# A hybrid decoder layer on one core: half-width recurrence levels, stores on ScalarE's queue, experts tile by tile, four sums held in PSUM

## The chip, the core and the metric

The kernel runs on one core of a Trainium2 chip. The metric is the time of one execution in device microseconds (us). The kernel before takes 2983.25 us, the median of three runs (2981.98 to 2986.4).

The text names the engines as the profile does: PE is TensorE (PEld its weight loads), DVE is VectorE, ACT is ScalarE, POOL is GpSimd, SP is SyncE, which here only issues DMAs (SPq).

## What is computed

One decoder layer over 1024 tokens of width 1024, float32 throughout:

```python
mod = silu(c) @ w_ada + b_ada              # shift/scale/gate of both sub-layers
h = rmsnorm(x) * (1 + scale1) + shift1
proj = h @ w_in
#  columns A: 4 heads x 128, gated linear recurrence with a decay per channel
#     scores[t, s] = sum_d q[t,d] k[s,d] exp(b[t,d] - b[s,d])   for s <= t in a chunk
#  columns B: 4 groups x 128, gated causal convolution of width 3
x = x + gate1 * (concat[A, B] @ w_out)
h = rmsnorm(x) * (1 + scale2) + shift2
#  PEER, per token: 8 heads, top 16 of 128 + 128 keys, top 16 of their sums -> 128 experts of 16384
act = gelu(h . u[expert]);  x = x + gate2 * sum(gate * act * v[expert])
out = rmsnorm(x) * final_norm_w
```

## The kernel before

**Products.** A float32 operand of a large product is split into a high part (a copy on ACT, line 113) and a low part (a subtraction on DVE, line 114); a product is then three matmuls (high.high, high.low, low.high). The weights come through one list `order` in the order of their use: SP loads a block of 512 KB into one of three buffers `wl` (line 201), ACT and DVE split it one or two blocks ahead of PE.

**Token mixing** (`mixing`) runs once for each half of the sequence, 24 blocks of `w_in` each (line 467), and between the blocks the recurrence of four heads. A chunk's 128x128 scores are built in levels: level l (0 to 6) covers the pairs (s, t) whose highest differing bit is l. `level(mask, X, Y)` multiplies four chunks of 128x128 on PE (line 577) and copies the pairs of its mask into `sT` with a predicated copy of 128x512 on DVE (line 578). A head has seven levels and the diagonal. Then the group norms' scales (`finish`, lines 681 and 683), the product with `w_out` (line 714), the residual and norm 2.

**PEER, dense and gathered.** 704 tokens of the second part take all 16384 experts in dense form; the other 320 ("gathered") read their own 128 expert rows each by indirect DMA, in tiles of 128, 128 and 64 tokens. The gathered tokens' queries come after the first half (line 873; scores and queries are stored in DRAM, lines 909 and 913).

**The background.** `background()` is a generator of steps on DVE and POOL: first the top-k of both full tiles (`top16`, `candidates`, `softmax`, `digits`, `pick`), which leaves their expert indices; then per tile 128 rows of `u`, each a gather by POOL (line 1082) and a product with accumulation on DVE (line 1100), and 128 rows of `v` (a gather, line 1092 on DVE), then the norm and the store (`norm_store`). `advance` draws steps in the midst of the other work, so many for each block and stage (`RATES`; the gates stage has 0). The planner that orders each engine's instructions may issue one earlier than its place in the program when its inputs are ready; the products with gathered rows are pinned behind the vector instruction traced before them. The gather of a row can run ahead as far as there are row buffers (five).

**Dense PEER.** Queries and top-k of the dense tokens, with blocks of `u` products (line 1161, two PSUM buffers `pa`, gelu on ACT at line 1166 into `ge`) strewn between; 40 of 128 such blocks are done early and their `ge` stored (`ged`, line 1174). The gates stage (`gates`) builds one-hot products (lines 1312 and 1318 on DVE), 16 matmuls for eight tokens (line 1327, five PSUM buffers `pg`), copies to `stg` on ACT (line 1330), and for each 64 tokens stores 4096 KB (`gd`, line 1335). The main loop takes the other 88 blocks, multiplies by the gates (line 1376), and for each three blocks runs `v_phase`: 16 sums of 128 x 384 or 128 x 320 (line 1395). Two of the sums stay in PSUM for the whole loop (`FIXED`), the other 14 are formed in one of four buffers `pv` and added to SBUF by DVE (line 1411).

**Queues.** SP issues nearly all loads and stores, in order; an issue waits for its buffer or its data and holds what is behind it. POOL issues the gathers and the stores of `x1d` and `h2d`.

Of the kernel before, what the change touches and what calls it, by code (L numbers as in the profile page):

```python
# [7 lines left out]
F32 = mybir.dt.float32  # L8
# [11 lines left out]
P = 128  # L20
# [19 lines left out]
# the gathered tokens of the last, half tile get their experts together with the half tile of the others  # L40
# [4 lines left out]
GB = 2  # L45
# [17 lines left out]
FIXED = [(0, 0), (1, 0)]  # L63
# [34 lines left out]
def build(tc, A, out, dbg=None):  # L98
# [27 lines left out]
    def rsqrt(r, v, tmp, e=0):  # L126
        """of v / 4 ** e: a first guess from the exponent, then Newton steps"""
# [12 lines left out]
    with root:  # L140
# [36 lines left out]
        # ---------------------------------------------------------------- stationary operands  # L177
        # all of [P, KC, P], in the order in which TensorE takes them; each is fetched two and split one ahead
# [24 lines left out]
        def halve(n):  # L203
            """there is a third set of halves at times"""
# [7 lines left out]
        def deepen(pl, first, n, every):  # L212
            """that many more from the first on: one of so many goes into a pool of its own"""
# [18 lines left out]
        def ahead():  # L232
            """in the midst of the products with one: split the next"""
# [5 lines left out]
        # ---------------------------------------------------------------- constants, modulation  # L239
# [4 lines left out]
        # three buffers of four row tiles, in turn of the normalised input or w_out, and of the mix or the residual  # L244
# [36 lines left out]
        # TensorE gets to its full clock while the first loads are under way  # L281
# [29 lines left out]
        def mod_part(sec, wa, d):  # L311
            """some columns of a section of the modulation"""
# [5 lines left out]
        def mod_part_rows(sec, wa, d):  # L318
            """the same on TensorE, as a row that is turned into columns"""
# [28 lines left out]
        # ---------------------------------------------------------------- norm 1 and the values  # L348
# [14 lines left out]
        def lnT1(xs, pl, k, h1, onact=False):  # L363
            """transpose a column block of the four row tiles, scale, shift and split it"""
# [16 lines left out]
        def wi_load(pl, k, lb=3, hb=2, ahead=0, wait=[]):  # L381
            """loads run ahead of the splits"""
# [34 lines left out]
        # ---------------------------------------------------------------- projections, token mixing  # L417
# [6 lines left out]
        # lower bounds  # L424
# [16 lines left out]
        # a window of 32 columns of it holds ones in one of them  # L441
# [12 lines left out]
        def mixing(half, mods, h1, og):  # L454
            """projections, recurrence, convolution and group norms of half a sequence, into og"""
# [43 lines left out]
            # blocks of w_in: per head f, q, g (0..11), per conv group c, x, b (12..23)  # L499
# [54 lines left out]
            # masks of the levels: the highest bit in which s and t differ, for s < t  # L554
# [14 lines left out]
            def hgrn(h):  # L569
# [3 lines left out]
                def level(mask, X, Y):  # L573
# [4 lines left out]
                    V.copy_predicated(sT, masks[mask][:, None, :].to_broadcast([P, HT, P]), ps_)  # L578
# [32 lines left out]
                level(7, kk, q)  # L611
                yield
                for l in range(6, -1, -1):
# [15 lines left out]
                    level(l, X, X)  # L629
# [42 lines left out]
            def finish(g):  # L672
                """the scales of a group, from the rows of all of them"""
# [18 lines left out]
        # ---------------------------------------------------------------- w_out, norm 2  # L692
# [840 lines left out]
```

## Time and profile before

| | |
|---|---|
| median of three runs | 2983.25 us |
| profiled execution, first to last instruction (span) | 2982.4 us |
| PE busy | 2902.0 us (97%) |
| DVE busy | 2524.2 us (85%) |
| ACT busy | 946.0 us (32%) |
| POOL busy | 796.2 us (27%) |
| DMA, mean rate | 238 GB/s, 709.65 MB |

The profile's page gives no other time of the profiled execution than its span; the median of the runs is 0.9 us above it. A busy PE is not PE at its peak, since matmuls overlap and their ends are modelled. The granted clock is 1.0 at 2.4 GHz and 0.5 at 1.2 GHz; a stretch's figure is the mean.

### The profile page before, as it was taken

How to read it: one execution, taken by the hardware profiler on the slowest of the kernel's cores; microseconds unless marked ns; L12 is line 12 of the kernel's file. 1: busy time of each engine (PE TensorE's matmuls, PEld its weight loads, DVE VectorE, ACT ScalarE, POOL GpSimd, SP SyncE). 2: the span in 40 equal slices, each digit the busy share in tenths (PEclk: the TensorE clock that was granted, in tenths of full speed). 3: DMA queues.
4: the chain of work that ended last, by engine and by line, in shares of the span. 5: the costliest groups of instructions: out<-in, count | busy, mean ns of one | idle time of the engine just before them, and what ended most of it. 6: DMA issues, size and time to landing. Idle time of an engine off the chain costs nothing.

```text
span 2982.4 us, 47131 instructions
## 1 busy us (share of the span) xinstructions
PE 2902.0 (97%) x18242; PEld 2750.8 (92%) x18242; DVE 2524.2 (85%) x5314; ACT 946.0 (32%) x1541; POOL 796.2 (27%) x661
## 2 busy tenths in 40 slices
PE   8999999999999999999999999999999999999998
PEld 6887888878999899999999999999999999999997
DVE  6885559988999877568889989889989988989987
ACT  5643655433122444422222222222222221222221
POOL 0000000000000000015454445435545444444450
PEclk8999999989999999999999999999999999999999
DMA  7424342244223577778889888889889888889883
GB/s 269 146 88 142 130 142 71 85 146 147 61 89 108 181 238 241 234 257 299 302 305 335 314 309 327 320 304 336 304 306 325 319 317 318 307 318 332 304 311 128
DMA packets 286898, 709.65 MB, mean 238 GB/s; under 512 B 26513, under 2 KB 124817, under 8 KB 284370
## 3 DMA queue, kind: packets, MB, share of 16 engines
q1 hardware_dynamic: 192994, 365.56, 35.5%
q0 software_dynamic: 93680, 341.09, 32.2%
q8 instruction: 142, 2.33, 0.3%
q14 instruction: 82, 0.67, 0.1%
HBM read 633.65 MB, written 72.88 MB: 237 GB/s over the span
## 4 chain that ended last, share of the span: by engine, by line
PE 64%; DVE 17%; DMA 10%; issue 5%; ACT 2%; POOL 1%; SPq 0%; DVEq 0%; ACTq 0%; POOLq 0%
PE pv L1395 22%; PE pa L1161 19%; PE pp L467 6%; DMA wl<-in_uT 5%; PE pq L873 4%; PE pacc L1395 3%; DVE wl L114 2%; DMA Wl<-ged 2%; PE ps L577 1%; PE pp L873 1%; PE pg L1327 1%; PE pp L378 1%; DVE gacc L1092 1%; PE pp L714 1%; DVE acc L1411 1%
## 5 line engine op out<-in xcount | busy, mean ns | idle before, releaser
L1161 PE MATMUL pa<-h2h,wh 128*128 128x384 f32 (+1 forms) x1840 | 598.4, 325 | 2.7 <-ACT ge L1166 2.6
L1161 PE MATMUL pa<-h2h,wl 128*128 128x384 f32 (+1 forms) x1840 | 593.9, 323 | 0.0
L1161 PE MATMUL pa<-h2l,wh 128*128 128x384 f32 (+1 forms) x1840 | 593.7, 323 | 0.0
L1395 PE MATMUL pv<-Wh,vh 128*128 128x384 f32 (+1 forms) x1792 | 580.6, 324 | 11.7 <-DVE acc L1411 11.1
L1395 PE MATMUL pv<-Wl,vh 128*128 128x384 f32 (+1 forms) x1792 | 577.3, 322 | 0.0
L1395 PE MATMUL pv<-Wh,vl 128*128 128x384 f32 (+1 forms) x1792 | 577.0, 322 | 0.0
L1395 PEld LDWEIGHTS pv<-Wh,vh 128*128 128x128 f32 x1792 | 336.9, 188 | 22.4 <-DVE acc L1411 19.6
L1161 PEld LDWEIGHTS pa<-h2h,wh 128*128 128x128 f32 x1840 | 346.0, 188 | 4.5 <-ACT ge L1166 3.8
L1161 PEld LDWEIGHTS pa<-h2l,wh 128*128 128x128 f32 x1840 | 346.2, 188 | 0.0
L1161 PEld LDWEIGHTS pa<-h2h,wl 128*128 128x128 f32 x1840 | 346.0, 188 | 0.3 <-DVE wl L114 0.3
L113 ACT ACTIVATE Wh<-Wl 128x704 fp32r<-128x704 f32 x128 | 101.6, 793 | 747.8 <-PE pv L1395 588.2
L1395 PEld LDWEIGHTS pv<-Wh,vl 128*128 128x128 f32 x1792 | 337.0, 188 | 0.0
L1395 PEld LDWEIGHTS pv<-Wl,vh 128*128 128x128 f32 x1792 | 336.9, 188 | 0.0
L113 ACT ACTIVATE wh<-wl 128x1024 fp32r<-128x1024 f32 x187 | 198.0, 1059 | 420.8 <-DMA wl<-in_uT 205.2
L114 DVE TENSOR_TENSOR wl<-wl,wh 128x1024 fp32r<-128x1024 f32 x187 | 227.8, 1218 | 97.7 <-ACT wh L113 95.9
L1411 DVE TENSOR_TENSOR acc<-acc,pv 128x320 f32<-128x320 f32 (+1 forms) x574 | 286.1, 513 | 11.6 <-PE pv L1395 11.3
L114 DVE TENSOR_TENSOR vl<-vl,vh 128x1024 fp32r<-128x1024 f32 x128 | 156.0, 1219 | 18.3 <-ACT vh L113 18.2
L113 ACT ACTIVATE vh<-vl 128x1024 fp32r<-128x1024 f32 x128 | 134.6, 1052 | 79.5 <-DMA vl<-in_v 45.4
L467 PE MATMUL pp<-h1h,wh 128*128 128x512 f32 x384 | 156.6, 408 | 0.0
L467 PE MATMUL pp<-h1h,wl 128*128 128x512 f32 x384 | 152.5, 397 | 3.5 <-DVE wl L114 3.4
L1376 DVE TENSOR_TENSOR Wl<-Wl,gsb 128x704 f32<-128x704 f32 x128 | 113.2, 885 | 48.4 <-DMA Wl<-ged 36.9
L467 PE MATMUL pp<-h1l,wh 128*128 128x512 f32 x384 | 152.3, 397 | 0.0
(1778 smaller groups left out, 5978.2 us busy)
## 6 DMA issues: line engine op xcount, KB each, us to landing
wl<-in_uT SPq DMA_DIRECT2D x128, 512.0 KB
vl<-in_v SPq DMA_DIRECT2D x128, 512.0 KB
gd<-stg SPq DMA_DIRECT2D x11, 4096.0 KB
gsb<-gd SPq DMA_DIRECT2D x64, 704.0 KB
wl<-in_win SPq DMA_DIRECT2D x48, 512.0 KB
wa<-in_wada SPq DMA_DIRECT2D x16, 1024.0 KB
wl<-in_wq SPq DMA_DIRECT2D x32, 512.0 KB
ged<-ge SPq DMA_DIRECT2D x40, 352.0 KB
```

Source lines behind the costliest of these rows:

```text
L113: C.activation(hi, src, AF.Copy)
L114: V.tensor_tensor(lo, src, hi.bitcast(F32), op=OP.subtract)
L378: T.matmul(pvs[t], l[:, t * P:(t + 1) * P], r, start=(k == 0 and l is h1[0][k] and r is wi[0]), stop=(k == KC - 1 and l is h1[1][k]))
L467: T.matmul(pp, l[:, k], r[k], start=(i == 0), stop=(i == 3 * KC - 1))
L577: T.matmul(ps_[:, c], X[:, cs_], Y[:, cs_], start=True, stop=True)
L714: T.matmul(pm, l[:, t * P:(t + 1) * P], r, start=(k == 0 and l is yh[k] and r is woh[k]), stop=(k == KC - 1 and l is yl[k]))
L873: T.matmul(pq[:, :m], l[:, k], hs[k, r][:, o:o + m], start=(i == 0), stop=(i == 3 * KC - 1))
L1092: V.scalar_tensor_tensor(ac, r, aw[:, j:j + 1], ac, op0=OP.mult, op1=OP.add))
L1161: T.matmul(pa[:, :n], l[:, k], h2[k, r][:, o:o + n], start=(i == 0), stop=(i == 3 * KC - 1))
L1376: V.tensor_tensor(gv, gv, gs[b // GB][:, :, b % GB], op=OP.mult)
L1395: T.matmul(pv[:, :n], l[:, c * P:(c + 1) * P], r[:, o:o + n], start=(i == 0 and (not fx or b0 == 0)), stop=(i == 3 * (b1 - b0) - 1 and (no ...
L1411: V.tensor_tensor(a, a, pv[:, :n], op=OP.add)
```

## The change

Comments aside, it has four parts.

1. `level` multiplies only the 64 columns t that can belong to a level (its upper halves). Levels 6 and 5 are copied into `sT` by ACT, block by block, without a mask; levels 4 to 0 by the predicated copy of 128x256. The diagonal is as it was.
2. The stores `scd`, `qgd`, `ged` and `gd` are issued by ACT in place of SP.
3. The background goes tile by tile: top-k of tile 0, its experts, top-k of tile 1, its experts, the last tile's experts. Its loads (`scd`, `h2d`, `x1d`, `g2d`, `fnw`) and its stores of `out` are issued by POOL in place of SP. `RATES` are as before.
4. Four sums stay in PSUM in place of two; the buffers of the other sums are in turn one of two `pa` and one of two `pv`.

```diff
-FIXED = [(0, 0), (1, 0)]
+FIXED = [(0, 1), (0, 5), (1, 1), (1, 5)]
...
+                def level(l, X):
+                    L = 1 << l
+                    n = P // (2 * L)
+                    Xv = X.rearrange("p (c n e l) -> p c n e l", n=n, e=2, l=L)
+                    sv = sT.rearrange("p c (n e l) -> p c n e l", e=2, l=L)[:, :, :, 1]
+                    ps_ = bank("ps")[:, :HT * P // 2].rearrange("p (c n l) -> p c n l", n=n, l=L)
+                    for c in range(HT):
+                        T.matmul(ps_[:, c], X[:, c * P:(c + 1) * P], Xv[:, c, :, 1], start=True, stop=True)
+                    if l >= 5:
+                        for i in range(n):
+                            r = slice(2 * i * L, (2 * i + 1) * L)
+                            C.activation(sv[r, :, i], ps_[r, :, i], AF.Copy)
+                    else:
+                        mv = masks[l].rearrange("p (n e l) -> p n e l", e=2, l=L)[:, :, 1]
+                        V.copy_predicated(sv, mv[:, None].to_broadcast([P, HT, n, L]), ps_)
...
-                SY.dma_start(scd[o:o + w, hp - 3:hp + 1], s_[:w, g])
+                C.dma_start(scd[o:o + w, hp - 3:hp + 1], s_[:w, g])
...
-            SY.dma_start(qgd[hp], qT[:, FULL * P:])
+            C.dma_start(qgd[hp], qT[:, FULL * P:])
...
         def background():
             for g in range(FULL):
+                yield from best(g)
+                yield from experts(g)
+            for g in range(FULL, NG):
+                yield from experts(g)
...
-                        SY.dma_start(s_, scd[g * P:(g + 1) * P, hp:hp + 4])
+                        G.dma_start(s_, scd[g * P:(g + 1) * P, hp:hp + 4])
...
-                    SY.dma_start(hx[c * w:(c + 1) * w], h2d[o:o + w])
+                    G.dma_start(hx[c * w:(c + 1) * w], h2d[o:o + w])
...
-                SY.dma_start(ged[e], ge)
+                C.dma_start(ged[e], ge)
...
-                SY.dma_start(gd[:, :, (t * P) // TG + q4].rearrange("g p b t -> p g b t"),
-                             stg.rearrange("p (g b) t -> p g b t", b=GB))
+                C.dma_start(gd[:, :, (t * P) // TG + q4].rearrange("g p b t -> p g b t"),
+                            stg.rearrange("p (g b) t -> p g b t", b=GB))
...
         def new_pv():
-            return psM.tile([P, 512], F32, name="pv", bufs=PV)
+            turn[0] ^= 1
+            if turn[0]:
+                return psU.tile([P, 512], F32, name="pa", bufs=2)
+            return psM.tile([P, 512], F32, name="pv", bufs=2)
```

## Rows read from the trace of the kernel before

**Rows 1.** The page: busy time of the engines; PE and granted clock in 40 slices; the chain that ended last, by engine.

```profile
PE 2902.0 (97%) x18242; PEld 2750.8 (92%) x18242; DVE 2524.2 (85%) x5314; ACT 946.0 (32%) x1541; POOL 796.2 (27%) x661
...
PE   8999999999999999999999999999999999999998
...
PEclk8999999989999999999999999999999999999999
...
PE 64%; DVE 17%; DMA 10%; issue 5%; ACT 2%; POOL 1%; SPq 0%; DVEq 0%; ACTq 0%; POOLq 0%
```

**Rows 2.** Busy time of each engine by stage: the stretch, its length, busy us (and instructions) of PE, PEld, DVE, ACT and POOL, granted clock, DMA share, GB/s. In order: mixing of the first half; its finish and `w_out` up to the residual; queries of the gathered tokens; mixing of the second half; its finish and `w_out` up to the residual; dense candidates and indices; gates; the last early blocks; main loop; end.

```profile
75.00:253.45 178.45, 177.73 (x988) 148.99 (x986) 143.47 (x261) 87.99 (x144) 0.00 (x0) 1.00 0.33 116
253.45:293.00 39.55, 37.93 (x171) 29.37 (x171) 20.72 (x34) 14.59 (x24) 0.00 (x0) 0.91 0.46 163
355.00:420.00 65.00, 62.66 (x429) 61.01 (x430) 20.33 (x20) 27.63 (x62) 0.00 (x0) 1.00 0.53 171
420.00:608.70 188.70, 183.51 (x986) 152.43 (x985) 184.27 (x677) 93.87 (x151) 2.23 (x3) 0.99 0.25 83
608.70:658.00 49.30, 42.89 (x177) 34.24 (x177) 37.84 (x100) 15.95 (x25) 5.03 (x4) 0.79 0.49 164
840.00:978.00 138.00, 131.55 (x794) 128.87 (x792) 134.59 (x595) 33.92 (x52) 0.76 (x1) 0.98 0.31 105
978.00:1260.00 282.00, 269.77 (x2514) 252.44 (x2513) 214.02 (x368) 137.47 (x258) 0.00 (x0) 0.99 0.74 226
1260.00:1280.00 20.00, 20.00 (x126) 19.93 (x125) 3.25 (x3) 3.99 (x7) 0.00 (x0) 1.00 0.99 326
1280.00:2940.00 1660.00, 1645.65 (x10188) 1632.69 (x10187) 1480.87 (x2084) 388.14 (x535) 781.08 (x634) 1.00 0.86 309
2940.00:2982.00 42.00, 33.01 (x223) 28.85 (x221) 28.76 (x94) 10.58 (x28) 0.00 (x0) 0.92 0.26 94
```

**Rows 3.** A level on PE and, for comparison, eight matmuls with a single moving column: instructions in order of time (start, us, engine, line; x16 are eight matmuls, each of two records).

```profile
486.06 1.95 PE L577 MATMUL ps<-X 128*128 128x128 f32 x16
...
766.04 1.95 PE L294 MATMUL sc<-ones,macc 128*128 128x1 f32 x16
```

**Rows 4.** Groups by line and shape (count, busy us, mean ns): the predicated copy of a level, a DVE operation of half its width, an ACT operation of half its width, the weights of the modulation on DVE.

```profile
L578 DVE COPY_PREDICATED sT<-mask,ps 128x512 f32<-128x512 int32 x64 | 47.3, 738 | 2.6 <-PE ps L577 1.9 <-PE po L634 0.6
...
L301 DVE SCALAR_TENSOR_TENSOR macc<-wa,cs,macc 128x1024 f32<-128x1024 f32 x28 | 35.6, 1273 | 0.1
...
L625 ACT ACTIVATE X<-X 128x256 f32<-128x256 f32 x56 | 23.6, 421 | 59.0 <-DVE X L621 58.9
L627 DVE TENSOR_TENSOR X<-X,kk 128x256 f32<-128x256 f32 x56 | 23.3, 417 | 3.0 <-ACT X L625 3.0
```

**Rows 5.** SP's issues in the gates stage, in order of time: a store of gates, and the issue that comes after it.

```profile
1020.85 0.37 SPq L1335 DMA_DIRECT2D gd<-stg  x1
1021.32 12.45 SPq L201 DMA_DIRECT2D wl<-in_uT  x1
...
1096.51 0.37 SPq L1335 DMA_DIRECT2D gd<-stg  x1
1098.49 11.30 SPq L1174 DMA_DIRECT2D ged<-ge  x1
...
1205.86 0.43 SPq L1335 DMA_DIRECT2D gd<-stg  x1
1214.92 5.45 SPq L1174 DMA_DIRECT2D ged<-ge  x1
```

**Rows 6.** Waits in the gates stage (978 to 1260): who waited for whom, us in total, times, longest; ACT's, then PE's.

```profile
ACT wh L113 <- DMA wl<-in_uT: 31.1, 10, 6.7
ACT wxh L113 <- DMA wl<-in_uT: 22.0, 6, 5.3
...
PE pg L1327 <- DVE P L1318: 9.4, 12, 2.6
```

**Rows 7.** The main loop: the additions of a sum on DVE and the two products with gathered rows (groups by shape), and the waits of PE, PEld and DVE between 1280 and 2940.

```profile
L1411 DVE TENSOR_TENSOR acc<-acc,pv 128x384 f32<-128x384 f32 x287 | 153.0, 545 | 0.2 <-PE pv L1395 0.2
...
L1411 DVE TENSOR_TENSOR acc<-acc,pv 128x320 f32<-128x320 f32 x287 | 133.2, 480 | 11.5 <-PE pv L1395 11.1
...
L1100 DVE SCALAR_TENSOR_TENSOR more<-more,hx 128x1024 f32<-128x1024 f32 x63 | 76.7, 1217 | 7.1 <-DMA more<-in_u,idx 7.1
...
PE pv L1395 <- DVE acc L1411: 11.1, 13, 2.1
...
PEld pv L1395 <- DVE acc L1411: 19.6, 30, 2.4
...
DVE grow__26105 L1100 <- DMA hx<-h2d: 3.5, 1, 3.5
```

**Rows 8.** The background's gathers on POOL, in order of time: the first, the last before the gap, the first after it (in brackets POOL's idle time before and what ended it).

```profile
592.95 1.01 POOL L1082 DMA_INDIRECT grow__13586<-in_u,idx  x1 [167.73 <-DVE hx L925]
...
652.22 0.94 POOL L1082 DMA_INDIRECT grow__13726<-in_u,idx  x1 [5.58 <-DVE grow__13586 L1100]
...
1303.88 1.02 POOL L1082 DMA_INDIRECT grow__13747<-in_u,idx  x1 [462.74 <-DVE grow__13654 L1100]
```

More of the change, by code (lines that the diff above doesn't have):

```diff
@@ L571, in hgrn, with diagonal @@
                 bf = b.rearrange("p c t -> p (c t)")
-                def level(mask, X, Y):
+                def diagonal(X, Y):
                     ps_ = bank("ps").rearrange("p (c t) -> p c t", t=P)
@@ L577, in level @@
                         T.matmul(ps_[:, c], X[:, cs_], Y[:, cs_], start=True, stop=True)
[L578 removed]
+                    V.copy_predicated(sT, masks[7][:, None, :].to_broadcast([P, HT, P]), ps_)
+                    advance(0.9 * RATES["B"])
+                def level(l, X):
[13 more added lines that the diff above has]
+                        V.copy_predicated(sv, mv[:, None].to_broadcast([P, HT, n, L]), ps_)
                     advance(0.9 * RATES["B"])
@@ L609, in states @@
                     yield
-                level(7, kk, q)
+                diagonal(kk, q)
                 yield
@@ L628, in hgrn @@
                     V.tensor_tensor(Xv[:, :, 1], Xv[:, :, 1], qv[:, :, 1], op=OP.mult)
-                    level(l, X, X)
+                    level(l, X)
                     yield
@@ L1000, in pick, with norm_store @@
                 yield 3.5
-        def norm_store(pl, o, w, parts, fw, r, sq):
+        def norm_store(pl, o, w, parts, fw, r, sq, queue=None):
             sf = pl.tile([P, 4], F32, name="sf", bufs=3)[:w]
@@ L1011, in norm_store @@
                 V.scalar_tensor_tensor(r[:w, sl], parts[j], sf[:, 2:3], fw[:w, sl], op0=OP.mult, op1=OP.mult)
-            SY.dma_start(out[o:o + w], r[:w])
+            (queue or SY).dma_start(out[o:o + w], r[:w])
         gp = pool(stQ, "gp", side="right")
@@ L1025, in background, with best @@
             for g in range(FULL):
+                yield from best(g)
+                yield from experts(g)
+            for g in range(FULL, NG):
+                yield from experts(g)
+        def best(g):
+            if True:
                 arenas = {a: [gp.tile([P, DM], F32, name=a, bufs=1), 0] for a in ("hx", "gacc", "more")}
@@ L1066, in background, with experts @@
                 V.tensor_copy(gkg[:, sl], gkf)
-            for g, (o, w) in enumerate(GG):
+        def experts(g):
+            if True:
+                o, w = GG[g]
                 c_ = dup(w)
@@ L1120, in background @@
                 x1 = gp.tile([P, DM], F32, name="hx", bufs=1)
-                SY.dma_start(x1[:w], x1d[o:o + w])
+                G.dma_start(x1[:w], x1d[o:o + w])
                 g2, fw = grow(), grow()
-                SY.dma_start(g2, bcast_rows(g2d[0]))
-                SY.dma_start(fw, bcast_rows(A["fnw"]))
+                G.dma_start(g2, bcast_rows(g2d[0]))
+                G.dma_start(fw, bcast_rows(A["fnw"]))
                 for j in range(2):
@@ L1350, in build @@
         fixed = {f: psM.tile([P, 512], F32, name=f"pacc{f[0]}{f[1]}", bufs=1) for f in FIXED}
-        PV = 6 - len(FIXED)
+        turn = [0]
         def new_pv():
-            return psM.tile([P, 512], F32, name="pv", bufs=PV)
+            turn[0] ^= 1
+            if turn[0]:
+                return psU.tile([P, 512], F32, name="pa", bufs=2)
+            return psM.tile([P, 512], F32, name="pv", bufs=2)
         foldps[0] = new_pv
```

2 lines of the change are left out of this document (1 added, 1 removed).

## The prediction, made before the change was run

> **What bounds the kernel now.** I read the page first [rows 1]: PE is busy for 97% of the span and makes 64% of the chain that ended last, DVE is at 85%. So an edit pays only where PE stands idle, or works at the low clock. The stages say where [rows 2]: length less PE's busy time is 14.4 us in the whole main loop (1660 less 1645.65), 12.2 in the gates, 9.0 at the end, 6.5 in the dense candidates, 6.4 in the second half's finish and w_out (at clock 0.79), 5.2 in its mixing. Everything the change can win is in these gaps. The reader should also see DVE's column: 184.3 of 188.7 us in the second half's mixing, but 143.5 of 178.5 in the first half's, which has the same 24 blocks.
>
> **Part 1, half-width levels.** On PE, the 16 records of a level of 128 columns take 1.95 us, and 16 records with one moving column take 1.95 us too [rows 3]. The time does not depend on the columns, so 64 of them cost what 128 did: 0 us. Were a halved matmul half as long, 448 records (the matmuls of the 56 levels of both halves) at 56 ns less each would give 25 us; were it longer through its strided columns, a loss. One column is the nearer row; I take 0.
>
> The Trainium skill (TensorE: Matmul & The Clock Gate, section Back-to-back issue gap) lists 134 cycles for 128 columns and about 60 for up to 64. By it the levels would give some 13 us on PE (estimate: 448 times 74 cycles at 2.4 GHz), and the sum below would be 13 us lower. The one-column rows of this trace speak against it.
>
> On DVE, of 64 copies of 0.738 us [rows 4] the diagonal's 8 stay, 16 go to ACT and 40 halve to about 0.42 (an operation of half the width takes 0.417): 11.8 + 12.7 = 24.5 us less, half of it in each mixing. ACT gets 24 copies of at most 0.42, 10 us in all, beside 88 and 94 us of work in stages of 178 and 189. In the first half PE lacks 0.7 us only: nothing. In the second half it goes into the next sum.
>
> **Part 3, tile by tile, in the second half.** Now the top-k of both tiles lies in the second half: gathers, which need its indices, begin at 593 and pause at 652 [rows 8]. Its price on DVE: mixing 184.3 less (143.5 less 27, the first half's 21 modulation steps of 1.273 [rows 4]) = 68; finish and w_out 37.8 less 20.7 = 17; 85 us for two tiles, 42 each. After the change tile 1's top-k needs the buffers of tile 0's experts and can't come before them. DVE in the mixing falls from 184 by 12 (levels) and some 35 to about 137 of 189, what the first half has. So PE's gap there should fall from 5.2 to the first half's 0.7: **-4.5 us**. The finish and w_out take 49.3 us against 39.55 for the same work without top-k, 9.75 more, part of it through the clock (0.79 against 0.91). Tile 0's rest may still fall there, so I take **-8** of it. Bounds of both together: 0 and -14.3.
>
> **Stores of the gathered queries.** 24 issues move to ACT, which has 27.6 us of work in 65; at SP's 0.37 to 0.43 each [rows 5] that is 10 us beside free time. SP's loads no longer stand behind stores. PE lacks 2.3 us: **-1** (0 to -2.3).
>
> **Dense candidates.** The program's places now put eight or so products with rows of tile 0 (1.22 + 0.08 us each, pinned) in this stage: about 10 us on a DVE that works 134.6 of 138. They stand ahead of candidates and indices, which the gates wait for; PE has early u blocks to fill with. Bounds 0 and +10; I take **+3**. A dozen more go with the last early blocks, where DVE does 3 us in 20, but the DMAs are at 0.99 and a gather may come late, ahead of the first gate products: **+1**, with bounds 0 and +8.
>
> **Part 2, stores in the gates stage.** Today the issue after a store of gates stands 5.5 to 12.5 us in SP's queue [rows 5], as long as the 4096 KB take to drain (about 13 us from 1020.85), and the weights' load is behind it or is itself held. ACT then waits for loads, 53 us in 16 waits, and PE lacks 12.2 us, 9.4 of them for one-hots of a DVE that is behind ACT [rows 2, 6]. With the stores in ACT's queue the loads go past them. I take half of the gap back, **-6** (bound -12). ACT's own new issues, 11 of gates and about 23 of ge at 0.4, are 14 us in a stage where it works 137 of 282. What is queued behind each on ACT: the next copies of `pg`, the gelus, the high parts of the next weights. This holds only if ACT itself is not held as SP was; that is the first rival.
>
> The Trainium skill (DMA: Bandwidth & Descriptors, section Issuing engines are not separate DMA queues) says that DMAs issued by another engine run on the same 16 engines, and that only sequencer time is saved. By it the loads would win nothing from going past, and this term would be 0 in place of -6. No row here has a store issued by ACT; SP's long issues show that sequencer time is just what was lost.
>
> **Part 4 and the main loop.** Two sums fewer go to SBUF in each of 41 phases: 82 additions of 0.513 (mean of 0.545 and 0.480 [rows 7]) = 42 us less on DVE. The 20 products moved ahead take 26 us away, tile 1's top-k brings 42. Net -26 of 1480.9, from 89% to 88% busy. PE's waits for these additions are 11.1 us; the waits for buffers stay as they are, four in turn before and after. Against it stand the changes of tile: `hx` and the first rows are queued on POOL behind the store of the last tile, which waits for its norm; DVE may stand some 5 us twice, against the 3.5 us wait for `hx` today. I take -4 for the first and +2 for the second: **-2** (bounds -11 and +10). The end keeps its chain: 0.
>
> **Sum.** -4.5 - 8 - 1 + 3 + 1 - 6 - 2 = -17.5 from the profiled 2982.4 gives 2964.9; with the 0.9 us by which the runs' median stands above that span, **2966 us**.
>
> **Rivals.**
> First, ACT is held in SP's place. The limit met SP's next issue whatever it was, and on ACT a store of `ge` follows each store of gates. The three ends [rows 5] give 5.5 to 12.5 us a hold; with 8.6 as their middle, 11 stores hold ACT for 95 us. Priced by today's exchange (53 us of waiting ACT for 12.2 of idle PE): 22 us, less the 12.2 that the loads stop costing, +10 in the stage. Priced as lumps: ACT's longest wait, 6.7 us, goes with PE's longest, 2.6 [rows 6], so some 4.1 us are covered, and 11 times the other 4.5 are 50, less 12, +38. In place of -6, the middle of +24 ends at 2996 us: slower. It decides from holds of about 4 us on. For it: the rows on SP. Against it: ACT is free for half of the stage, PE has five `pg` and two `pa` to run ahead, and 16 such waits of ACT have cost PE little more than half a microsecond each.
>
> Second, the main loop pays. Tile 1's top-k, which is not pinned, comes in a clump on a DVE at 88%, as in the second half, where 85 us of it cost PE 14.3: 7 us for 42; and each change of tile stands 5 us longer than taken, less some cover. About +12: 2978 us. For it, PE does wait for DVE there now; against it, DVE is relieved by 42 us in just this loop.
>
> Third, the change doesn't do what it says: DVE's freed time in the second half is filled again, since tile 0's softmax and indices fall due at its finish. Then the -12.5 stays out: 2978 us. Against it: 42 us of top-k in place of 85.
>
> **How the numbers follow.** Forecast 0.55, with its own range 2950 to 2977; ACT held 0.25; the main loop pays 0.12; the second half stays 0.08. All good ends together (-4.5, -9.8, -2.3, 0, 0, -12.2, -11) give 2943; the first rival at its middle, 2996, and 10 of the 14 us to its upper price give the other end: range **2942 to 3006**. A difference of 0.2%, 6 us, is about what a measurement of this kernel can tell. Faster by more: nearly all of the forecast (0.53), a tenth of the first rival, a quarter of the others: 0.61. Within: a fifth of the first rival, half of the others, a little of the forecast: 0.16. Slower: the rest of the first rival and some of the second: 0.23.
>
> **What would show it.** Right: level matmuls at the old 1.95 us for 16; no DVE top-k of tile 1 before the main loop; the second half's finish and w_out at about 41 us; no long issue on SP in the gates stage, and PE's gap there at half. Wrong: ACT's queue with issues of 5 us and more behind `gd<-stg`, followed by PE waiting for gelus and `pg`; DVE over 95% in the dense candidates with PE idle; PE waits for DVE's additions in the main loop above 11 us.

## The result, and the profile after

The changed kernel takes **3003.8 us** (median of five runs, 2996.8 to 3008.7) against 2983.3 for the kernel before in the same session: a ratio of **1.0074, interval 1.0054 to 1.0095** (here and below the ratio is estimated from all runs of both kernels, not from the two medians). The forecast was 2966 us, with a range of 2942 to 3006. The time lies inside the range and on the other side of the sign.

The page of the changed kernel (span, busy time, and the chain that ended last, by engine):

```profile
span 3004.6 us, 46958 instructions
...
PE 2907.6 (97%) x18242; PEld 2764.1 (92%) x18242; DVE 2475.7 (82%) x5210; ACT 953.7 (32%) x1567; POOL 806.0 (27%) x685
...
PE 46%; DVE 6%; DMA 5%; issue 2%; ACTq 1%; ACT 1%; POOL 0%; SPq 0%; DVEq 0%; POOLq 0%
```

DVE lost 48.5 us of work and the kernel got longer, so what this relief won is less than what was lost elsewhere. `ACTq`, ScalarE's own issues, has 1% of the chain, where [rows 1] has 0%; the other shares can't be compared, since those shown here add up to 61% of the span and those of [rows 1] to 99%. By stage the profile reads as follows (columns as in [rows 2]; each stretch now runs from PE's first record of the stage to its first of the next: mixing of the first half, gathered queries, second mixing, its finish and `w_out` with norm 2, dense candidates, gates, last early blocks, main loop):

```profile
63.00:259.50 196.50, 195.70 (x1062) 163.97 (x1060) 147.58 (x278) 99.28 (x166) 0.00 (x0) 0.98 0.36 123
351.90:421.80 69.90, 66.53 (x454) 65.31 (x452) 21.94 (x21) 31.30 (x72) 1.59 (x3) 0.98 0.50 162
421.60:620.50 198.90, 191.94 (x1027) 159.34 (x1025) 160.28 (x500) 96.49 (x167) 11.69 (x12) 0.98 0.28 91
620.50:688.10 67.60, 61.44 (x265) 49.49 (x265) 44.38 (x104) 29.47 (x60) 2.21 (x4) 0.88 0.45 148
837.30:992.60 155.30, 147.15 (x884) 145.00 (x884) 152.19 (x638) 40.61 (x64) 10.76 (x9) 0.97 0.40 132
992.60:1275.80 283.20, 257.19 (x2400) 239.96 (x2400) 210.12 (x356) 130.86 (x247) 1.64 (x1) 0.97 0.70 215
1275.80:1311.00 35.20, 28.64 (x170) 28.06 (x169) 12.49 (x21) 6.75 (x11) 10.68 (x10) 0.90 0.99 339
1311.00:2983.40 1672.40, 1657.85 (x10302) 1650.84 (x10303) 1478.87 (x2248) 398.37 (x554) 764.13 (x635) 1.00 0.86 303
```

The second mixing and the gates stage of the kernel before, cut in the same way:

```profile
417.00:612.70 195.70, 190.28 (x1027) 157.88 (x1025) 189.82 (x707) 96.12 (x157) 2.23 (x3) 0.99 0.25 84
...
985.30:1255.10 269.80, 259.90 (x2460) 242.93 (x2459) 207.23 (x351) 134.13 (x249) 0.00 (x0) 1.00 0.75 229
```

Blocks of `u` move between neighbouring stages (the gates stage has 60 PE records fewer than before, the candidates 58 more), so lengths mislead. The measure used from here on is **PE's lost time**: over all PE records of a stage, the distance from one start to the next, less the distance that its form keeps when nothing disturbs it (173 ns for 384 columns, 146 for 320, 60 for the gates' one-hots, 112 for short float32 products). It counts idle time, and also the low clock and late starts after a wait. In us, one profiled execution each:

| stage | before | changed | e1 | e2 | e3 | e5 | e6 | e7 | e10 | e11 | e12 |
|---|---|---|---|---|---|---|---|---|---|---|---|
| first mixing | 7.3 | 10.6 | 10.7 | 8.9 | 8.3 | 10.7 | 11.4 | 11.4 | 7.3 | 7.3 | 8.2 |
| gathered queries | 3.9 | 6.1 | 6.0 | 6.2 | 3.2 | 6.7 | 6.0 | 3.8 | 1.9 | 4.4 | 3.1 |
| second mixing | 15.1 | 18.4 | 17.3 | 15.3 | 15.7 | 17.3 | 16.1 | 18.1 | 18.0 | 14.9 | 15.2 |
| finish, `w_out`, norm 2 | 25.2 | 16.3 | 16.4 | 17.8 | 25.8 | 16.4 | 28.5 | 15.6 | 16.3 | 24.4 | 24.2 |
| dense candidates | 15.9 | 14.9 | 15.1 | 14.9 | 14.0 | 14.8 | 14.7 | 14.5 | 14.7 | 14.2 | 15.9 |
| gates | 18.1 | **40.9** | 18.8 | 25.1 | **31.2** | 19.1 | 19.3 | 19.4 | 13.8 | 17.9 | 16.6 |
| last early blocks | 1.1 | 9.8 | 11.8 | 10.7 | 2.0 | 5.2 | 2.6 | 13.3 | 8.2 | 1.8 | 4.3 |
| main loop | 33.8 | 26.6 | 18.3 | 21.9 | 26.7 | 30.0 | 13.2 | 36.1 | 23.3 | **17.0** | 27.7 |

From before to changed the rows give +3.3, +2.2, +3.3, -8.9, -1.0, +22.8, +8.7 and -7.2, together +23.2; the spans differ by 22.2 (PE began 1.0 us earlier). One execution each leaves noise in the table: the runs of the kernel before spread from 2969 to 2988 us, and kernels with the same main loop differ in that row by 7 to 8 us (before 33.8, e3 26.7, e12 27.7; changed 26.6, e1 18.3, e2 21.9). A few us in one cell decide nothing there.

The greater part of the loss sits in the gates stage. Its first cause is in ScalarE's own queue (ACT and its issues, ACTq, of the changed kernel in order of time: start, us, engine, line; in brackets the idle time before):

```profile
1102.98 0.44 ACT L1197 ACTIVATE ge<-pa 128x320 f32<-128x320 f32 x1 [0.74 <-PE pa L1192]
1103.31 1.05 ACT L113 ACTIVATE wh<-wl 128x1024 fp32r<-128x1024 f32 x1
1103.45 13.17 ACTq L1205 DMA_DIRECT2D ged<-ge  x1
1116.72 1.57 ACT L1361 ACTIVATE stg<-pg 128x512 f32<-128x512 f32 x3 [12.35 <-issue]
```

The 4 MB store of gates was issued at 1102.26. The next issue on ACT, a 352 KB store of `ge`, stands 13.17 us, and behind it ACT does nothing for 12.35 us, "issue" being the releaser. PE then waits for the engine that should empty its buffers (waits of the gates stage and the last early blocks, PE's and then ACT's, changed kernel):

```profile
PE pg L1358 <- ACT stg L1361: 16.8, 8, 6.4
PE pg L1358 <- DVE P L1349: 7.1, 10, 2.9
PE pa L1192 <- ACT ge L1197: 6.5, 1, 6.5
...
ACT stg L1361 <- issue: 32.9, 4, 12.4
ACT wh L113 <- issue: 27.5, 3, 12.2
...
ACT wxh L113 <- issue: 15.2, 2, 8.1
```

In [rows 6] PE waited for DVE alone, and ACT for loads. Now SP has no long issue left and ACT's waits for loads of weights are down to 3.5 us, but it stands behind its own queue for 75.6. Eleven issues of `ge` were held for 4.0 to 13.2 us, 89.6 us in all (the last of them in the stretch of the last early blocks).

### The profile page after: what moved, and what is told of

It reads as the page before. It is cut to its first block, busy times and chain, and to the rows that moved or that the text cites. A ratio compares the mean times of both kernels' runs of the same rounds, so it can differ in the third digit from the quotient of the medians.

```text
span 3004.6 us, 46958 instructions
## 1 busy us (share of the span) xinstructions
PE 2907.6 (97%) x18242; PEld 2764.1 (92%) x18242; DVE 2475.7 (82%) x5210; ACT 953.7 (32%) x1567; POOL 806.0 (27%) x685
## 4 chain that ended last, share of the span: by engine, by line
PE 46%; DVE 6%; DMA 5%; issue 2%; ACTq 1%; ACT 1%; POOL 0%; SPq 0%; DVEq 0%; POOLq 0%
PE pa L1192 20%; PE pv L1431 10%; PE pa L1431 10%; PE pacc L1431 6%; DMA wl<-in_uT 2%; DMA Wl<-ged 1%; DVE acc L1447 1%; DVE wl L114 1%; ACTq L1205 1%; PE pg L1358 1%; DVE vl L114 1%; DVE gacc L1123 1%; ACT wh L113 0%; DVE Wl L1412 0%; DMA vl<-in_v 0%
## 5 line engine op out<-in xcount | busy, mean ns | idle before, releaser
L1192 PE MATMUL pa<-h2h,wh 128*128 128x384 f32 (+1 forms) x1840 | 602.5, 327 | 12.2 <-ACT ge L1197 10.7
L1431 PE MATMUL pa<-Wh,vh 128*128 128x384 f32 (+1 forms) x768 | 248.6, 324 | 7.6 <-ACT Wl L1197 5.0
L1431 PE MATMUL pv<-Wh,vh 128*128 128x384 f32 (+1 forms) x768 | 247.7, 322 | 1.1 <-DVE acc L1447 1.0
L1431 PE MATMUL pa<-Wl,vh 128*128 128x384 f32 (+1 forms) x768 | 247.7, 322 | 0.2 <-DVE Wl L114 0.2
L1431 PE MATMUL pv<-Wl,vh 128*128 128x384 f32 (+1 forms) x768 | 247.1, 322 | 0.0
L1431 PE MATMUL pa<-Wh,vl 128*128 128x384 f32 (+1 forms) x768 | 247.0, 322 | 0.0
L1431 PE MATMUL pv<-Wh,vl 128*128 128x384 f32 (+1 forms) x768 | 246.9, 322 | 0.0
L1113 POOL DMA_INDIRECT more<-in_u,idx x63 | 81.5, 1294 | 401.8 <-DVE more L1131 326.1
L114 DVE TENSOR_TENSOR vl<-vl,vh 128x1024 fp32r<-128x1024 f32 x128 | 156.2, 1221 | 16.6 <-ACT vh L113 16.6
L1431 PE MATMUL pacc<-Wh,vh 128*128 128x384 f32 (+1 forms) x512 | 165.0, 322 | 3.3 <-ACT vh L113 3.3
L1431 PE MATMUL pacc<-Wh,vl 128*128 128x384 f32 (+1 forms) x512 | 164.7, 322 | 0.8 <-DVE vl L114 0.8
L1431 PE MATMUL pacc<-Wl,vh 128*128 128x384 f32 (+1 forms) x512 | 164.6, 322 | 0.0
## 6 DMA issues: line engine op xcount, KB each, us to landing
gd<-stg ACTq DMA_DIRECT2D x11, 4096.0 KB, 17.8
```

The lines of the kernel that those rows point to most:

```text
L1113: G.indirect_dma_start(out=r, out_offset=None, in_=src, in_offset=IndirectOffsetOnAxis(ap=idx[:n, s0 + j:s0 + j + 1], axis=0))
L1192: T.matmul(pa[:, :n], l[:, k], h2[k, r][:, o:o + n], start=(i == 0), stop=(i == 3 * KC - 1))
L1431: T.matmul(pv[:, :n], l[:, c * P:(c + 1) * P], r[:, o:o + n], start=(i == 0 and (not fx or b0 == 0)), stop=(i == 3 * (b1 - b0) - 1 and (no ...
```

## The experiments

The kernels e1 to e4, e5 to e8 and e9 to e12 each ran as a group beside the same runs of the kernel before; ratios are against those.

**e1: the stores of `ge` back on SP.**

```diff
-                C.dma_start(ged[e], ge)
+                SY.dma_start(ged[e], ge)
```

> The changed kernel with one edit: the stores of ge go back to SP, the 4 MB stores of gates stay on ScalarE. Held queue: in the changed kernel 11 stores of ge stood 4.0 to 13.2 us in ScalarE's queue behind a store of gates, 90 us in all, and PE's idle time in the gates stage was 26 us and 6.6 in the last early blocks, against 9.9 and 0.8 before. With the stores of ge on SP nothing follows a store of gates on ScalarE for 19 us or more, so no issue is long on either queue, PE's idle time in both stages falls below 10 us together, and the kernel takes 2968 to 2978 us. Rival, the stage itself: the time went through the order of the loads and of the early blocks in this stage, not through the queue; then 2998 to 3008 us. Second rival, the hold belongs to the store and not to the queue: SP's stores of ge stand 5 us and more although the gates' store is on another queue; then about 2983 us.

Measured 2978.0 us, ratio 0.9999 (0.9985 to 1.0012). The second rival falls: no issue on either queue reached 1.5 us between 980 and 1320. The gates stage's lost time went from 40.9 to 18.8. The time fell to the top of the forecast for a held queue, and no further, because the wait ahead of the main loop was not ACT's queue (PE's waits of gates and early blocks in e1):

```profile
PE pacc L1431 <- ACT vh L113: 11.5, 1, 11.5
PE pg L1358 <- DVE P L1349: 4.9, 8, 1.7
PE pg L1358 <- DVE O L1343: 2.7, 4, 1.1
```

**e2: the stores of gates back on SP, those of `ge` left on ACT.**

```diff
-                C.dma_start(gd[:, :, (t * P) // TG + q4].rearrange("g p b t -> p g b t"),
+                SY.dma_start(gd[:, :, (t * P) // TG + q4].rearrange("g p b t -> p g b t"),
```

> The changed kernel with one edit: the 4 MB stores of gates go back to SP, the stores of ge stay on ScalarE. Held queue: ScalarE has no issue above 1 us, SP's next issue after each store of gates, now a load of weights, stands 5 us and more as in the kernel before, PE's idle time in the gates stage comes back to 10 to 14 us, and the kernel takes 2976 to 2988 us. Rival, the stage itself: 2998 to 3008 us, since the loads again stand behind the stores or the order stays.

Measured 2985.1 us, ratio 1.0016 (1.0002 to 1.0030). ACT had no long issue; SP had eleven, all loads of weights, 112 us in all, and PE's lost time in the gates stage was 25.1 against e1's 18.8. The time lies inside the forecast. So a hold seems to cost something on SP too when the load itself is next in the queue, but less than on ACT (18.8 to 40.9). By what path is not shown: PE's waits there are for DVE's one-hots (12.4 us for `P`, 4.9 in e1).

**e3: the kernel before, with both kinds of store on ACT and nothing else.**

```diff
-                SY.dma_start(ged[e], ge)
+                C.dma_start(ged[e], ge)
...
-                SY.dma_start(gd[:, :, (t * P) // TG + q4].rearrange("g p b t -> p g b t"),
+                C.dma_start(gd[:, :, (t * P) // TG + q4].rearrange("g p b t -> p g b t"),
```

> The kernel before with one edit: its stores of gates and of ge are issued by ScalarE. Held queue: about 11 stores of ge are held 4 to 13 us in ScalarE's queue, the gates stage and the last early blocks grow by 20 to 31 us together, all other stages stay, and the kernel takes 3002 to 3014 us, as much as or more than the changed kernel. Rival, the loss came from the other parts of the change (half-width levels, order of the background): 2977 to 2990 us.

Measured 2994.9 us, ratio 1.0046 (1.0030 to 1.0061), some 14 us slower: the sign and the place are right (31.2 us lost in the gates stage; eleven holds, 79 us), the size is below the forecast. The gates stage lost 13.1 us more than in the kernel before, where the changed kernel lost 22.8 more, and the last early blocks stayed at 2.0. No gather runs beside the last store here, and its hold ended 14.5 us after the store's issue; in the changed kernel, beside gathers, it ended after 19.7. Why the other ten holds cost PE less here stays open.

**e4: level products over 128 columns again, copies of half width.**

```diff
-                        T.matmul(ps_[:, c], X[:, c * P:(c + 1) * P], Xv[:, c, :, 1], start=True, stop=True)
+                        T.matmul(pf_[:, c], X[:, cs_], X[:, cs_], start=True, stop=True)
```

> The changed kernel with one edit: TensorE forms the level products over all 128 columns again, and only the copies out of PSUM are of half width. In the changed kernel each mixing is 3.2 us longer than before, PE's records of levels start every 112 ns as before, and stretches at the low granted clock follow runs of level products and of one-column products (0.80, 0.77 and 0.58 in 4 us windows at 200, 204 and 240 us), where before the first mixing had none. Columns theory: fewer columns in the products cost the granted clock; with 128 the first mixing comes back to 1.00 and 193 to 194 us, the second to 195 to 197, and the kernel is 4 to 7 us faster than the changed one, 2997 to 3000 us. Rival, waits: the dips come from how copies and exponentials are shared between VectorE and ScalarE; then no difference, 3001 to 3006 us.

Measured 2999.2 us, ratio 1.0066 (1.0050 to 1.0081): inside the forecast, but not told apart from the changed kernel's 1.0074. The stages speak more clearly. The first mixing came back to 193.5 us and a granted clock of 1.00, as expected; the second went the other way, to 203.9, with PE waiting up to 3.04 us for ACT and DVE.

**e5: e1 without background along the last early blocks.**

```diff
-RG = 0.5
+RG = 0.0
```

> The kernel of e1_ge_sp with one more edit: the background takes no step along the last early blocks (its rate there is 0), so no row of an expert is gathered between the last gate products and the main loop. In e1_ge_sp the last 4 MB store of gates took 29 us from issue to landing beside these gathers, where the others take 17 to 18; the first load of gates and the loads of weights behind it in SP's queue left only then, and PE stood 11.6 us ahead of its first product of the main loop. Theory, gathers delay the last store: its landing comes back to 17 to 19 us, the stretch from the last gate product to the main loop goes from 38.2 to 28 to 31 us, and the kernel is 6 to 10 us faster than e1_ge_sp, 2966 to 2973 us. Rival, the wait at the main loop's start has another cause (the early blocks run down, the store is late anyway): 2975 to 2981 us.

Measured 2984.8 us, ratio 1.0011 (0.9997 to 1.0025): no gain against e1. The stretch did shrink, from 38.2 to 31.6 us, and PE's wait ahead of the main loop from 11.5 to 4.9. The forecast of 6 to 10 us less is missed. The main loop's lost time rose from 18.3 to 30.0 with new waits, the longest 3.9 us for DVE's `Wl`. What was won at its start was given back in it; that the rows moved into it did this is possible, not shown.

**e6: e1 with the top-k of both tiles first.**

```diff
-                yield from best(g)
-                yield from experts(g)
-            for g in range(FULL, NG):
+                yield from best(g)
+            for g in range(NG):
                 yield from experts(g)
```

> The kernel of e1_ge_sp with the order of the background undone: the top-k of both tiles of gathered tokens comes first, as in the kernel before, then the experts. Theory, the second half's finish and w_out paid for top-k: its stretch, 76.7 us before and 67.7 in e1_ge_sp, goes back to 75 to 78, the last early blocks lose their gathers' delay only if the background is then behind its due (0 to 10 us back), the main loop gains 0 to 5 us of VectorE's time; together 2972 to 2988 us, with the w_out stretch as the test. Rival, that stretch became shorter through the half-width levels: it stays at 67 to 69.

Measured 2976.4 us, ratio 0.9993 (0.9978 to 1.0007). The test of the theory holds: the stretch with `w_out` went from 67.7 to 79.8 us, somewhat past the forecast. Against these 12 us stand 9 in the last early blocks and 5 in the main loop, so going tile by tile won its 9 to 12 us and lost as much elsewhere.

**e7: e1 with two sums in PSUM and four `pv` buffers.**

```diff
-FIXED = [(0, 1), (0, 5), (1, 1), (1, 5)]
+FIXED = [(0, 0), (1, 0)]
...
-            turn[0] ^= 1
-            if turn[0]:
-                return psU.tile([P, 512], F32, name="pa", bufs=2)
-            return psM.tile([P, 512], F32, name="pv", bufs=2)
+            return psM.tile([P, 512], F32, name="pv", bufs=PV)
```

> The kernel of e1_ge_sp with the main loop's sums as before: two of them stay in PSUM, and four buffers of their own take turns for the rest. Theory, four sums pay: PE's lost time in the main loop, 33.8 us before and 18.3 in e1_ge_sp, comes back to 25 to 34, VectorE gets 82 additions or 42 us more there, and the kernel is 6 to 14 us slower than e1_ge_sp, 2984 to 2992 us. Rival, the main loop's gain came from the order of the background: it stays within 4 us of e1_ge_sp's.

Measured 2998.4 us, ratio 1.0062 (1.0045 to 1.0079): 19 us slower than e1, beyond the forecast. The main loop's lost time doubled to 36.1. The main loop's part was the change's best. The edit moves two things at once, how many sums stay in PSUM and which buffers the others use; the runs do not separate them, here or in e11.

**e8: e5 with the half-width levels undone** (`level` and the diagonal as in the kernel before).

> The kernel of e5_no_gathers_early with the half-width levels undone: products and copies of all 128 columns as before. Theory, the levels cost the two mixings time (196.6 and 197.8 us in e1_ge_sp against 193.2 and 195.7 before; first mixing with 128 column products 193.5): the mixings are 2 to 6 us shorter together, and the kernel is that much faster than e5_no_gathers_early. Rival, the copies' saving of VectorE's time is worth more: 2 to 8 us slower.

Measured 2979.1 us, ratio 1.0002 (0.9988 to 1.0016) against e5's 1.0011: the intervals overlap, so the time does not decide between the theory and its rival. The first mixing was 3.5 us shorter (193.1 against 196.6), the second 0.8 longer.

**e11: the kernel before with four sums alone** (the edit of e7, turned round).

> The kernel before with the main loop's part of the change alone: four sums stay in PSUM, and the others take the two pa buffers and two pv buffers in turn. Theory, four sums pay by themselves: PE's lost time in the main loop was 33.8 us in the kernel before and 36.1 in e7_two_sums, 13.2 and 18.3 in the two kernels with four sums and gathers along the last early blocks; here it falls to 15 to 26, all other stages stay, and the kernel is 8 to 18 us faster than before. Rival, the gain needs the order of the background as well: within 5 us of before.

Measured **2966.5 us, ratio 0.9957 (0.9940 to 0.9973)**, 13 us faster than before: the best of all kernels run. The main loop went from 1677.5 to 1661.8 us (its row, with the columns as above):

```profile
1279.70:2941.50 1661.80, 1656.86 (x10302) 1650.60 (x10303) 1462.01 (x2042) 395.62 (x551) 778.66 (x634) 1.00 0.87 309
```

PE's waits in it:

```profile
PE pa L1399 <- ACT Wl L1166: 3.0, 3, 2.5
PE pacc L1399 <- ACT vh L113: 1.3, 2, 1.0
PE pa L1161 <- DVE acc L1415: 1.1, 1, 1.1
```

PE's wait for additions, 11.1 us in 13 times in [rows 7], is down to 1.1 in one. In e3 and e12, whose main loop is that of the kernel before, it is 9.1 and 7.9 us.

**e12: the kernel before with the stores of gates alone on ACT.**

> The kernel before with its 4 MB stores of gates alone on ScalarE; nothing else moves. No queue then has an issue that stands behind such a store. Theory of the prediction, SP's holds (11 issues, 95 us in all) cost PE 6 us or more of its 12 us of idle time in the gates stage: 2972 to 2977 us where before stands at 2981. Rival, weights are fetched so far ahead that the holds on SP cost nothing, and PE's waits there are VectorE's one-hots: within 3 us of before, lost time of the stage 17 to 20 us as before (18.1; 18.8 in e1_ge_sp).

Measured 2984.0 us, ratio 1.0017 (1.0005 to 1.0028). The prediction's theory falls: no queue has a long issue any more, and nothing is won; by the interval some 2 to 8 us are lost. The eleven issues on SP, held for 95.5 us in the kernel before, are all short, and ACT's waits for loads of weights in the gates stage and the last early blocks fell from 49.8 to 23.6 us. PE got 1.5 us of that: the gates stage lost 16.6 us in place of 18.1, the last early blocks 4.3 in place of 1.1. What PE waits for in the gates stage is what it waited for before, DVE's one-hots, 8.4 us in place of 9.4:

```profile
PE pg L1327 <- DVE P L1318: 6.6, 9, 2.5
PE pg L1327 <- DVE O L1312: 1.8, 3, 0.8
PE pa L1161 <- ACT ge L1166: 1.1, 1, 1.1
```

**e9 and e10: two combinations.** e9 is e6 with the old levels; e10 is e1 with the old levels and one constant moved:

```diff
-NF = 2.1
+NF = 2.0
```

> Both kernels' better parts: stores of gates on ScalarE, stores of ge on SP, four sums in PSUM, background loads on GpSimd, the top-k of both tiles first and whole-width levels as in the kernel before. From e6_best_first (2976 us), whose first mixing was 3.5 to 4 us longer than with whole-width products: 2969 to 2975 us, 6 to 14 faster than before. Rival, the levels cost nothing in sum: 2974 to 2980.

> The kernel of e1_ge_sp with whole-width levels, and with 2.0 early blocks along each store of gates in place of 2.1, so that about one block more of TensorE's work (8 to 9 us) is left for the stretch in which the last store of gates lands beside the gathers. Theory, only that landing ends last there: PE's wait of 11.6 us ahead of the main loop falls to 2 to 5 us, the gates stage gets shorter by the block that leaves it, and the kernel takes 2964 to 2972 us. Rival, the gates stage lacks the block as cover for VectorE's one-hots: its lost time grows from 18.8 to 25 and more, and the time stays at 2973 to 2980.

e9 took 2973.8 us, ratio 0.9977 (0.9965 to 0.9989), at the upper end of its forecast, where its rival begins, so it does not decide between the two; it won less than the four sums alone. e10 took 2968.3, ratio 0.9965 (0.9953 to 0.9977), inside its forecast. The rival fell, as the gates stage lost 13.8 us, less than e1's 18.8. With 219 PE records left for the last early blocks in place of 168, their lost time was 8.2 in place of 11.8; PE's wait ahead of the main loop fell from 11.5 to 8.0 us only, where 2 to 5 were forecast. Most of the 10 us against e1 lie elsewhere (the gates stage lost 5.0 us less, the gathered queries 4.1, the first mixing 3.4); how they divide between the two edits is not shown.

## Why the prediction was wrong, point by point

**The step that failed** is the -6 for the stores in the gates stage ("With the stores in ACT's queue the loads go past them. I take half of the gap back"), and the choice behind it, 0.55 against 0.25, that ACT would not be held as SP was. The rival that was written down, ACT held in SP's place, is what happened, and the prediction's own sign of being wrong was seen (issues of 5 us and more behind `gd<-stg`, then PE waiting for `pg` and gelus): it counted 95 us of holds and a middle of +24 for the stage; measured were 89.6 us and +22.8. That the size fits so well is partly luck, as +24 was the middle of two prices, +10 and +38, and the same move alone gave +13.1 (e3). Undoing the hold alone gives 22 us back (e1, 1.0074 to 0.9999), and making it alone costs the kernel before 14 (e3).

Two of the arguments against that rival were misread. "ACT is free for half of the stage" counts busy time, where a hold asks for slack at one moment. The 176 copies of the stage came one each 1.6 us, so five `pg` last some 8 us (an estimate); a hold of 10 us outlasts them. "16 such waits of ACT have cost PE little more than half a microsecond each" were waits of 53 us in all, 3.3 on average and 6.7 at most, not holds of 8.1 on average and 13.2 at most.

The other half of the step was wrong by itself. SP's holds cost the kernel before nothing that can be seen: without any hold (e12) its gates stage keeps its lost time to 1.5 us. ACT's waits for loads, 53 us in [rows 6], were about halved and PE gained next to nothing, so they were covered; and the 9.4 us for one-hots, which the prediction laid to a DVE behind ACT, shrank by 1 us only.

The rule that was weighed there, the Trainium skill's in DMA: Bandwidth & Descriptors, section Issuing engines are not separate DMA queues (another issuing engine saves sequencer time and nothing else), would have put 0 in place of -6, and e12 agrees with it: the time was not gained (ratio 1.0017). What the rule does not speak of, e3 shows: the hold goes along with the store, to an engine that has work to do.

The other terms, against the table:

- **Levels on PE, 0.** Right as far as the spacing goes: the median distance of two level records is 112 ns with 64 columns as with 128. The 13 us that were estimated from the Trainium skill's table (TensorE: Matmul & The Clock Gate, section Back-to-back issue gap) did not appear. Not foreseen was the clock, below: about +3 us in the first mixing. On DVE the copies of half width saved 19 us of the 24.5, since 16 of the 40 did not get shorter at all (last section).
- **Second mixing, -4.5.** Wrong: +3.3. DVE fell from 189.8 to 160.3 us, though not to 137, and PE's gap did not follow. PE's longest waits there were on chains within a block: 1.75 us for `X` from DVE (line 647), 1.38 for `kd` from ACT (line 614). DVE's busy share was no measure of this gap. In the four kernels that left the levels and the background alone (before, e3, e11, e12) the stage took 195.3 to 196.3 us, in the others 195.9 to 203.9; which part of the change makes it longer stays open.
- **Finish and `w_out`, -8.** Right: -8.9, and e6 shows that top-k was the cause. e6 also shows that it is paid back.
- **Gathered queries, -1.** Right where the products have 128 columns: with these stores on ACT the stage loses 1.9 to 2.0 us (e4, e8, e9, e10), without 3.1 to 4.4. But it is +2.2 in the changed kernel, by a wait of 2.2 us for ACT's `qT` behind a split that waits for its load. The level products are not in this stage; why their width goes with that wait is not shown.
- **Dense candidates, +3.** Nothing: -1.0.
- **Last early blocks, +1 (0 to +8).** Mis-sized, and for other reasons than given: +8.7, and +10.7 in e1. PE waited for no gathered row there. In the changed kernel 6.5 us of it are the failed step once more, PE's wait for `ge` behind ACT's last hold, which ran beside gathers and ended 19.7 us after its store's issue (ACT and its queue, then PE):

```profile
1276.53 0.38 ACTq L1366 DMA_DIRECT2D gd<-stg  x1
1283.64 12.57 ACTq L1205 DMA_DIRECT2D ged<-ge  x1
1296.34 1.06 ACT L113 ACTIVATE wh<-wl 128x1024 fp32r<-128x1024 f32 x1 [12.21 <-issue]
...
1297.77 0.64 PE L1192 MATMUL pa<-h2h,wh 128*128 128x320 f32 x1 [6.47 <-ACT ge L1197]
```

  Where the hold is gone, the last store of gates itself comes late, and every first load of the main loop stands behind it on SP. In e1 (POOL, then SP, in order of time; the store was issued on ACT at 1252.39):

```profile
1256.79 0.94 POOL L1113 DMA_INDIRECT grow__13198<-in_u,idx  x1 [0.30 <-issue]
1266.58 1.68 POOL L1113 DMA_INDIRECT more<-in_u,idx  x1 [8.85 <-DVE more L1131]
...
1265.20 0.33 SPq L201 DMA_DIRECT2D wl<-in_uT  x1
1281.46 0.80 SPq L1408 DMA_DIRECT2D gsb<-gd  x2
1282.31 0.42 SPq L1417 DMA_DIRECT2D vl<-in_v  x1
```

  `gsb<-gd` waits for the store's landing until 1281.46, and `vl`, whose high part PE waits for, leaves after it.
- **Main loop, -2.** Mis-sized: the four sums alone are worth 13 us of the whole time (e11), and the stage's lost time falls by 16.8 (by 10 to 11 from e3 and e12, which have the old main loop too). The -4 for the additions was taken below the 11.1 us of waits, as if these were all that could be won. Lost time shows more: in the kernel before, records behind a wait for additions lost 14.3 us, and some 70 further records that were not idle started late and lost about 7.5; that the additions delayed these too is likely, as in e11 such losses fell to about half. The changed kernel got 7.2 us, no more than kernels with the same main loop differ by. The second rival, the main loop as payer, did not come: its DVE top-k of tile 1 stands there from 1912 to 1976 and PE's waits remain below 2 us each, behind a first wait of 3.3 us.

## What to carry to other kernels

Before a large store is moved to another engine's queue, ask what the next issue on that queue is and what that engine computes in between: here the holds behind 4 MB stores were harmless in the kernel before on an engine that only issues (e2 leaves open whether they always are), and cost 14 to 22 us on one that empties PSUM. A stage's waits show which of its stalls end anything: removing 95 us of held issues was worth nothing, while keeping two more sums in PSUM, which takes away 82 additions behind 11 us of PE's waits, was worth 13. And parts of one change should be timed alone, since the best of them was here hidden by the worst.

## What the runs showed of the hardware

**The hold belongs to the issuing queue.** The issue after a 4 MB store of gates stood until 13.0 to 15.3 us after that store's issue on ACT (ten of eleven; 19.7 for the last, beside gathers); there it was always a store of `ge`. The kernel before shows the same on SP, for loads and stores alike (12.9, 13.3 and 14.5 us for the three pairs of [rows 5]). Issues on the other queue were free at the same time: in e1, with the stores of gates on ACT, no issue of SP reached 1.5 us.

**How long the last store takes depends on what passes it.** From its issue to the first load that waits for it:

| gathers issued in between | us |
|---|---|
| 0, loads held behind the store on SP (before, e11) | 16.9 |
| 0, ACT held behind the store (e3) | 17.4 |
| 0, store on ACT, loads on SP free (e6, e9, e12) | 20.0 to 20.2 |
| 3 (e4, e5, e8, changed) | 20.5 to 22.6 |
| 6 to 7 (e1, e2, e7) | 28.2 to 29.1 |
| 9 (e10) | 34.0 |

In e3, e4 and the changed kernel the load left 0.5 us behind a load of weights; the stores had landed after 16.8, 21.7 and 22.1 us. Transfers that go past the store make it land later: with SP's loads and stores going past 3 us later, with six to nine gathers beside it 11 to 17. So a freed queue can take back at the stage's end what it gives within.

**The level products of half width cost the clock.** In all six kernels with products of 64 columns the first mixing took 194.8 to 197.1 us at a granted clock of 0.98 to 0.99; in the eight with 128 columns 193.1 to 194.1 at 0.99 to 1.00. In the changed kernel the clock falls after a run of short products (windows of 4 us; the granted clock is the third column from the right):

```profile
196.00:200.00 4.00, 4.00 (x25) 3.44 (x23) 1.97 (x6) 0.66 (x1) 0.00 (x0) 1.00 0.46 131
200.00:204.00 4.00, 4.00 (x30) 4.00 (x31) 3.32 (x7) 0.40 (x1) 0.00 (x0) 0.80 0.01 4
204.00:208.00 4.00, 4.00 (x19) 3.50 (x18) 2.62 (x6) 2.33 (x5) 0.00 (x0) 0.77 0.43 131
```

PE's short products there, in order of time:

```profile
198.81 1.00 PE L589 MATMUL ps<-X 128*128 128x64 f32 x8
199.65 1.89 PE L294 MATMUL po<-ones,macc 128*128 128x1 f32 x16
201.40 0.91 PE L577 MATMUL ps<-q,kk 128*128 128x128 f32 x6
202.15 0.83 PE L653 MATMUL po<-sT,vt 128*128 128x128 f32 x4
202.78 0.63 PE L655 MATMUL po<-qe,Ss 128*128 128x128 f32 x2
```

From 202.4 us on, short records that start 112 ns apart elsewhere start 213 ns apart, with the clock granted at 0.5, the level of 1.2 GHz, although PE had not been idle. In the kernel before, the windows 200 to 204 and 204 to 208 have 1.00. Halved products kept the spacing and lost the clock; e4, which differs from the changed kernel in these products and in where the copies read them, has 1.00 again. Below level 6 the 64 columns also stand in runs with gaps between, the 128 do not; whether their number or the gaps count is not shown.

**A copy of half width is shorter only if its columns stand in runs.** The predicated copies of 128x256 took 553 ns on average against 738 for 128x512, but no copy took 553. For the levels 4, 3 and 2, whose columns stand in runs of 16, 8 and 4, they took 418 to 453 ns, about the 0.42 us that were forecast; for the levels 1 and 0, with runs of 2 and 1, they took 715 to 748, as long as a whole copy. The group, and one head of the changed kernel from level 4 to level 0:

```profile
L597 DVE COPY_PREDICATED sT<-mask,ps 128x256 f32<-128x256 int32 x40 | 22.1, 553 | 11.0 <-PE ps L589 9.0 <-ACT wh L113 1.1
...
90.49 0.43 DVE L597 COPY_PREDICATED sT<-mask,ps 128x256 f32<-128x256 int32 x1
98.96 0.42 DVE L597 COPY_PREDICATED sT<-mask,ps 128x256 f32<-128x256 int32 x1
100.14 0.42 DVE L597 COPY_PREDICATED sT<-mask,ps 128x256 f32<-128x256 int32 x1
105.89 0.74 DVE L597 COPY_PREDICATED sT<-mask,ps 128x256 f32<-128x256 int32 x1 [1.47 <-PE ps L589]
112.36 0.74 DVE L597 COPY_PREDICATED sT<-mask,ps 128x256 f32<-128x256 int32 x1
```

In e4, which copies the same columns out of products of full width, the two groups are the same (409 to 444 and 719 to 740 ns).
